# Block products for the first feed-forward matrix, on normalised rows, and the last norm's squares summed on VectorE

## The chip, the cores and the metric

The kernel runs on one core of a Trainium2 chip. The core has a matrix engine (TensorE, PE in the profile, with PEld for its weight loads), a vector engine (VectorE, DVE), an activation engine (ScalarE, ACT), GpSimd (POOL), and queues that issue DMAs (SP is SyncE's). The metric is the device time of one execution in microseconds; three runs of the kernel before gave 1327.4, 1327.84 and 1328.44 us, median 1327.84 us.

## What is computed

One step of a decoder layer in float32, for 512 prompt rows and 8 sample rows, 520 columns together. The change concerns the end of it:

```python
h = h + mix                                   # mix: everything up to w_o
h = h + swiglu(rmsnorm(h, ln2_g), w_ffn_in, w_ffn_out)
y = rmsnorm(h, lnf_g)

def swiglu(xn, w_ffn_in, w_ffn_out):
    a, b = split(xn @ w_ffn_in, 2)            # each 2816 wide = 22 blocks of 128
    return (silu(a) * b) @ w_ffn_out          # model width 1024 = 8 blocks of 128
```

## The kernel before

**Layout.** Activations stand transposed: model channels on the 128 partitions, in 8 blocks `c`, and 520 columns in two halves of 260 (`HF`). A float32 product is made of three products of a rounded high part and a remainder: weight high by data high, weight high by data low, weight low by data high (`product`, L237). Weights arrive in 194 tiles of eight 128x128 blocks (`raw`, 512 KB, four buffers); ScalarE copies 512 columns into the high part `wh` (L195), VectorE subtracts for the low part `wl` (L198). This is done five such blocks ahead of their use (`AHEAD`, called from `advance`).

**A unit.** `unit` (L252) multiplies 8 weight blocks with a full tile: 8 x 3 x 2 halves = 48 matmuls of 260 columns, into a pair of PSUM banks `pm`, of which there are two (tag `pm`, used in turn). After each `k`, `pump` lets side generators emit one piece of work and runs work put off with `later(n, ...)` by n pumps. Order in each engine's queue is the order in which the program emits; nothing is re-sorted.

**A quad.** `quad` (L266) does two output blocks against eight input blocks by seven block products instead of eight (Strassen's scheme in Winograd's form): seven blocks `j`, each 4 x 3 matmuls, 84 in all. Seven sums of weights are made on VectorE by `block_sum` (1024, 512 and 512 columns), seven high and low parts are split, and the right side's four sums come from `right` (L292): four VectorE operations of 260 columns, one ScalarE copy of 1820 columns, and a VectorE subtraction of 1820 columns put off by three pumps. Three banks are used: bank 0 for j = 0, 2, 4, 6, bank 1 for j = 1, 5, and `pc` for j = 3. After j = 0, 1, 2, 4 ScalarE copies the bank to a side tile (`snap`, L289), because the next block product is accumulated on top of it. So j = 2 may not start before the copy after j = 0 has read the bank, j = 4 not before that after j = 2, j = 6 not before that after j = 4.

**The feed forward before.** `ffn_in(i)` makes hidden block i of 22: one unit for `a`, one for `b`, on `X2`, which is h times the norm's gain, split in two, *without* the row factor. The factor `rs2` (1/rms of each column) is applied when the banks are read: VectorE multiplies `a` (L1209), ScalarE takes Silu (L1210), VectorE multiplies `b` (L1215) and the two (L1220). Every odd i up to 15 then runs `right` on the pair; blocks 17 to 21 are split plainly (`whole`, L1201). `ffn_out(c)` multiplies the hidden blocks with the second matrix, by quads, for two chunks of eight hidden blocks; the third chunk of six is plain. The order is: hidden 0 to 8, four quads, hidden 9 to 16, four quads, hidden 17 to 21, the plain end. `rs2` itself comes from `gen_norm2`, which runs under the first units: VectorE has both halves of it late in the second unit.

**The end.** The third chunk's output is first made for c = 0 to 3 whole, then for c = 4 to 7 half by half. `gen_final(c)` squares h (ScalarE), transposes h on TensorE (`fin_T`, three transposes), sums squares with three small matmuls against a column of ones (`fin_ss`, L1277 and L1279), and VectorE multiplies the transposed rows by the gain (`fin_g`, L1283). In the last half, after the first matmuls of c = 6, everything pending is drained and `fin_out(0)` finishes the first half of the rows; `fin_out(1)` ends the program.

Of the kernel before, what the change touches and what calls it, by code (L numbers as in the profile page):

```python
# [27 lines left out]
QUADS = {s + 2 * i: 4 for s in (146, 170) for i in range(4)}  # L28
# [4 lines left out]
def tile_hybrid_layer(  # L33
# [204 lines left out]
    def product(pm, n, k, nk, src, fs):  # L238
        h, l = split[bid[n // 8, n % 8 // 4]]
        j = n % 4  # L240
        wh, wl = h[:, j * 128:(j + 1) * 128], l[:, j * 128:(j + 1) * 128]
        xh, xl = src(k)
        for w, x, first, last in ((wh, xh, k == 0, False), (wh, xl, False, False), (wl, xh, False, k == nk - 1)):
            for f in fs:
                PE.matmul(pm[:, f, :HF], w, x[:, f * HF:(f + 1) * HF], start=first, stop=last)  # L245
# [4 lines left out]

    def unit(nk, src, evac=None):
        pm = pmain.tile([128, 2, 512], F32, tag="pm", name="pm")  # L252
# [13 lines left out]
    def quad(odd, xh, xl, snap, evac):  # L266
# [5 lines left out]
        pms = [pmain.tile([128, 2, 512], F32, tag="pm", name="pm")[:, 0, :HF] for _ in range(2)]  # L272
        out = (pms[::-1] if odd else pms) + [None]
# [162 lines left out]
    for h in range(RH):  # L436
# [245 lines left out]
        for which in ("q", "k"):  # L682
            e0, e1 = rot(which)
            if h == 0 and which == "q":
                pattern[:] = ["P"]
                push("P", gen_norm1())
                pms = [pmain.tile([128, 2, 512], F32, tag="pm", name="pm") for _ in range(2)]
# [482 lines left out]

    def gen_norm2():
# [10 lines left out]
        for f in range(2):  # L1182
# [3 lines left out]
            yield  # L1186


    pattern[:] = ["P"]
    push("P", gen_norm2())  # L1190

    UH = bpool.tile([128, 28, HF], F32R, tag="bg", name="UH")
    UL = fp.tile([128, 28, HF], F32R, name="UL")
    UF = fp.tile([128, 8, HF], F32, name="UF")
    UH4, UL4 = (u.rearrange("p (k x) c -> p k x c", x=7) for u in (UH, UL))
    UHp, ULp = (u.rearrange("p (k f) c -> p k (f c)", f=2) for u in (UH, UL))
    NP = CHUNKS[2][0]

# [4 lines left out]

    def ffn_in(i):
        s = {}

        def ev_fa(pm, s=s):
            t = ftmp("fa")
            V.tensor_tensor(halves(t), pm, halves(rs2), op=ALU.mult)  # L1209
            A.activation(t, t, AF.Silu)  # L1210
            s["a"] = t

        def ev_fb(pm, i=i, s=s):
            t = ftmp("fb")
            V.tensor_tensor(halves(t), pm, halves(rs2), op=ALU.mult)  # L1215
            if i > NP:
                V.tensor_tensor(t, t, s["a"], op=ALU.mult)
                whole(i, halves(t))
                return
            V.tensor_tensor(UF[:, 1:3, :] if i % 2 else UF[:, 0::7, :], halves(t), halves(s["a"]), op=ALU.mult)  # L1220
            if i % 2:
                k = i % 8 // 2
                right(UF, UH4[:, k], UL4[:, k])

        pa = unit(8, lambda k: (X2[:, k, :], X2[:, 8 + k, :]), ev_fa if i else None)
        pb = unit(8, lambda k: (X2[:, k, :], X2[:, 8 + k, :]), ev_fb if i else None)
        if i == 0:
            drain("P")
            ev_fa(pa)
            ev_fb(pb)  # L1230

    def ffn_out(c):

        s12 = fp.tile([128, 2, HF], F32, tag="s12", bufs=2, name="s12")
        s35 = fp.tile([128, 2, HF], F32, tag="s35", bufs=2, name="s35")
# [14 lines left out]
        quad(c // 2 % 2, UH4, UL4, [s12[:, 0, :], s12[:, 1, :], s35[:, 0, :], s35[:, 1, :]], evac)  # L1250

    for (a, n), ahead in zip(CHUNKS, (1, 1, 0)):
        if not ahead:
            whole(NP, UF[:, 0::7, :])
        for i in range(a and a + 1, a + n + ahead):
            ffn_in(i)
        if ahead:
            for c in range(0, 8, 2):
                ffn_out(c)

    yt = bpool.tile([128, 4, D], F32, tag="bx", name="yt")
    ys = fp.tile([4, 2, D], F32, name="ys")
    gb = fp.tile([128, D], F32, name="gb")
# [11 lines left out]
    def fin_ss(c, f, sq):  # L1275
        for j in range(2):
            PE.matmul(ssb[:, 2 * f + j:2 * f + j + 1], sq[:, 128 * j:128 * j + 128], ones1, start=c + f + j == 0, stop=c == 7,  # L1277
                      skip_group_check=True)
        PE.matmul(ssb[:4, 4 + f:5 + f], sq[:, HT:HF], ones1, start=False, stop=c == 7, skip_group_check=True)  # L1279
# [6 lines left out]

    def gen_final(c, fs=(0, 1)):
        sq = ftmp("sqf")
        A.activation(sq[:, :HF * len(fs)], hT[:, c, HF * fs[0]:HF * fs[-1] + HF], AF.Square)
        for f in fs:  # L1290
            for _ in range(2 if f else 4):
                yield
            a = fin_T(c, f)
            fin_ss(c, f, sq[:, HF * (f - fs[0]):])
            yield
            fin_g(c, f, *a)
            if f != fs[-1]:
# [32 lines left out]
    pms = [pmain.tile([128, 2, 512], F32, tag="pm", name="pm") for _ in range(2)]  # L1330
    base = pos[0]
    for i, (c, k) in enumerate(LAST):
# [3 lines left out]
        if k == nk - 1:  # L1336
            ev_f(pms[c][:, :, :HF], c)
            push("P", gen_final(c))
    pos[0] = base + len(LAST)
    for c in (2, 3):  # L1340
        unit(nk, usrc, lambda pm, c=c: ev_f(pm, c))
        push("P", gen_final(c))
    base = pos[0]
    for f in range(2):
        for c in range(4, 8):
            o = pmain.tile([128, 2, 512], F32, tag="pm", name="pm")[:, :1, :]
            for k in range(nk):
# [10 lines left out]
                if f and c == 6 and k == 0:  # L1358
# [3 lines left out]
            if c < 7:  # L1362
                push("P", gen_final(c, (f,)))
# [44 lines left out]
def _layout(np, i):  # L1408
# [14 lines left out]
    ffi = ff[[j for c in range(NFF) for j in (c, NFF + c)]].reshape(NFF, 16, 128, 128)  # L1423
    fo = _tiles(f["w_ffn_out"][0])

    def quad(w, c, a):
# [37 lines left out]
```

## Time and profile before

| what | value |
|---|---|
| median of three runs | 1327.84 us |
| the profiled execution | 1326.3 us, of it span 1324.5 us |
| VectorE busy, 20 us from 1073 to 1083 and 1043 to 1053 | 4.17 and 9.07 us of 10 |
| first unit of the feed forward | from about 926.4 us |
| the four quads of the first chunk | about 1033 to 1074 us |
| those of the second chunk | about 1166 to 1206 us |
| plain end of the second product | from about 1264 us |
| last output DMA issued | about 1321 us |

The busy time of an engine says how much of a stretch it had an instruction in work; an engine can be far from full over the span and full in one stage. Each engine takes its queue in order, so an instruction that waits also holds what is behind it. The rows of the profile stand in the prediction, beside what is read from them.

### The profile page before, as it was taken

What the parts mean: (1) busy time and instruction counts of PE and PEld (TensorE: products, weight loads), DVE (VectorE), ACT (ScalarE), POOL (GpSimd) and SP (SyncE); (2) the same over time, 40 slices, a digit from 0 to 9 for tenths busy, and PEclk for the clock granted to TensorE, in tenths of its full rate; (3) what the DMA queues carried; (4) which work ended last, traced back from release to release, by engine and by line L of the source; (5) the groups of instructions that cost most, each with busy time, mean ns of one, the idle gap of its engine ahead of it and who ended that gap; (6) DMA issues with size and microseconds to landing.
All of it is one profiled execution on the core that took longest, in us unless ns stands there. A gap on an engine that the chain in (4) does not pass through costs nothing.

```text
span 1324.5 us, 25798 instructions
## 1 busy us (share of the span) xinstructions
PE 1303.2 (98%) x10681; PEld 1272.9 (96%) x10681; DVE 753.6 (57%) x1582; ACT 527.1 (40%) x984; POOL 83.6 (6%) x69
## 2 busy tenths in 40 slices
PE   8999999999999999999999999999999999999997
PEld 7999999998888999999999999999999999999997
DVE  7867636747655532234545455486455865586443
ACT  4564334535553522243434433233333543354321
POOL 3601001001002000000000000040000000000000
PEclk9999999999999999999999999999999999999998
DMA  6266235746485233444645546534232333223211
GB/s 217 84 234 227 89 118 201 232 134 229 156 295 158 89 96 96 133 132 147 181 135 171 152 142 220 167 119 133 72 106 80 94 101 110 80 88 120 86 43 66
DMA packets 89782, 183.37 MB, mean 138 GB/s; under 512 B 12024, under 2 KB 33944, under 8 KB 89664
## 3 DMA queue, kind: packets, MB, share of 16 engines
q1 hardware_dynamic: 88944, 180.64, 42.7%
q8 instruction: 84, 1.38, 0.4%
q10 hardware_dynamic: 720, 1.07, 0.2%
q14 instruction: 34, 0.28, 0.1%
HBM read 155.70 MB, written 25.98 MB: 137 GB/s over the span
## 4 chain that ended last, share of the span: by engine, by line
PE 89%; DVE 4%; DMA 3%; issue 1%; ACT 1%; POOL 1%; SPq 0%; DVEq 0%; ACTq 0%
PE pm L245 70%; PE pm L283 5%; PE sp L308 3%; DMA vb<-vd 2%; PE sp L537 2%; PE sp L555 2%; PE pm L1355 2%; PE sp L947 1%; PE sp L489 1%; PE pc L283 1%; DVE wl L198 1%; PE sp L897 1%; PE sacc L1092 1%; DVE X L408 0%; PE sp L886 0%
## 5 line engine op out<-in xcount | busy, mean ns | idle before, releaser
L245 PE MATMUL pm<-X,wh 128*128 128x260 f32 x4608 | 755.9, 286 | 3.9 <-DVE X L340 3.6
L245 PEld LDWEIGHTS pm<-X,wh 128*128 128x128 f32 x4608 | 636.0, 189 | 18.2 <-issue 8.2
L245 PE MATMUL pm<-X,wl 128*128 128x260 f32 x2304 | 464.6, 283 | 0.0
L198 DVE TENSOR_TENSOR wl<-raw,wh 128x512 fp32r<-128x512 f32 x384 | 275.1, 720 | 209.0 <-ACT wh L195 206.9
L245 PEld LDWEIGHTS pm<-X,wl 128*128 128x128 f32 x2304 | 356.0, 189 | 0.0
L195 ACT ACTIVATE wh<-raw 128x512 fp32r<-128x512 f32 x384 | 237.9, 625 | 242.0 <-PE pm L245 186.0
L245 PE MATMUL pm<-GA,wh 128*128 128x260 f32 x512 | 82.2, 283 | 0.0
L245 PEld LDWEIGHTS pm<-GA,wh 128*128 128x128 f32 x512 | 70.1, 188 | 0.0
L317 POOL TENSOR_TENSOR r<-v,cst 128x4 f32<-128x4 f32 (+4 forms) x14 | 17.6, 1260 | 603.2 <-DVE v L315 603.2
L605 ACT ACTIVATE kv<-vb,ks 128x512 f32<-128x512 f32 x64 | 44.2, 714 | 27.9 <-DMA vb<-vd 27.5
L283 PE MATMUL pm<-UH,wh 128*128 128x260 f32 x192 | 54.4, 283 | 0.1
L283 PE MATMUL pm<-UH,wl 128*128 128x260 f32 x192 | 54.3, 283 | 0.0
L283 PE MATMUL pm<-UL,wh 128*128 128x260 f32 x192 | 54.3, 283 | 0.0
L640 DVE SCALAR_TENSOR_TENSOR st<-st,kv 128x512 f32<-128x512 f32 x64 | 45.4, 713 | 11.1 <-ACT kv L605 11.0
L245 PE MATMUL pm<-GA,wl 128*128 128x260 f32 x256 | 51.6, 283 | 0.0
L1210 ACT ACTIVATE fa<-fa 128x520 f32<-128x520 f32 x22 | 14.1, 639 | 71.3 <-DVE fa L1209 71.3
L245 PE MATMUL pm<-M,wh 128*128 128x260 f32 x256 | 41.1, 282 | 0.0
L245 PEld LDWEIGHTS pm<-GA,wl 128*128 128x128 f32 x256 | 39.5, 188 | 0.0
L283 PEld LDWEIGHTS pm<-UH,wh 128*128 128x128 f32 x192 | 36.2, 189 | 0.5 <-issue 0.5
L283 PEld LDWEIGHTS pm<-UL,wh 128*128 128x128 f32 x192 | 36.2, 188 | 0.0
L283 PEld LDWEIGHTS pm<-UH,wl 128*128 128x128 f32 x192 | 36.1, 188 | 0.0
L865 DVE SCALAR_TENSOR_TENSOR area<-area 128x128 f32<-128x128 f32 x96 | 22.7, 290 | 22.5 <-DMA area<-qd 22.5
(280 smaller groups left out, 1549.5 us busy)
## 6 DMA issues: line engine op xcount, KB each, us to landing
raw<-wall SPq DMA_DIRECT2D x192, 512.0 KB
st<-state SPq DMA_DIRECT2D x64, 256.0 KB
out<-st SPq DMA_DIRECT2D x64, 256.0 KB
area<-ck SPq DMA_DIRECT2D x24, 512.0 KB
vb<-vd SPq DMA_DIRECT2D x32, 256.0 KB
area<-qd SPq DMA_DIRECT2D x12, 512.0 KB
cb<-cd SPq DMA_DIRECT2D x4, 768.0 KB
xr<-xT SPq DMA_DIRECT2D x8, 260.0 KB
```

What stands on the lines that cost most here:

```text
L195: A.activation(h, r, AF.Copy)
L198: V.tensor_tensor(l, r, f32(h), op=ALU.subtract)
L245: PE.matmul(pm[:, f, :HF], w, x[:, f * HF:(f + 1) * HF], start=first, stop=last)
L283: PE.matmul(out[bank], w[:, ks], r[:, k, x, :], start=bank not in begun, stop=k == nkp - 1 and r is xh and w is l, skip_group_check=True)
L308: PE.transpose(out, in_, ident[:n, :n])
L317: G_.tensor_tensor(r[:rows, :ncol], v[:rows, :ncol], mhalf[:rows].to_broadcast([rows, ncol]), op=ALU.pow)
L537: PE.matmul(sp[:, i0:], v[x][:, jb, c * 128:(c + 1) * 128], scs[y][:, SCO[jb]:SCO[jb] + T - i0], start=jb == 0 and x == y, stop=jb == 3 an ...
L555: PE.matmul(sp, kt[x][:, jb, dt * 128:(dt + 1) * 128], v[y][:, jb, :], start=jb == 0 and x == y, stop=jb == 3 and x == 1)
L605: A.activation(kvs[i][:, :DV], vbs[b], AF.Copy, scale=ks[:, dt, b:b + 1])
L640: V.scalar_tensor_tensor(sts[i], sts[i], GAMMA[h], kvs.pop(i)[:, :DV], op0=ALU.mult, op1=ALU.add)
L865: V.scalar_tensor_tensor(pr[:, e], kb[:, e], 1.0, qb[:, e], op0=ALU.mult, op1=ALU.mult, accum_out=Ss[:, g, 32 * h + b:32 * h + b + 1])
L1355: PE.matmul(o[:, 0, :HF], w[:, js], x, start=k == 0 and i == 0, stop=k == nk - 1 and i == 2)
```

## The change

Twelve hidden blocks (5, 6, 8, 9, 11, 12, 14, 15, 17, 18, 20, 21) take `a` and `b` together by one `quad` (84 matmuls) in place of two units (96). For that the right side must be the eight input blocks in Winograd's form, and because the results of block products are subtracted from each other and read straight from PSUM, the rows are normalised beforehand: `gen_factors` makes `XH`/`XL` (7 + 1 slots for each of four pairs) from h, gain and `rs2`. Blocks 0 and 1 still run on `X2`, blocks 2, 3, 4, 7, 10, 13, 16, 19 run plainly on the plain slots of `XH`/`XL`, without the multiplication by `rs2`. `UH` moves to `X2`'s place, `XH` takes the place that `UH` had; the residual tiles `xr` now share a ring of five with the temporaries (two and six before); the tile `s35` has one buffer. At the end the squares are summed by VectorE into `ssa`, and only two sums per half go through TensorE; a final's transposes start two pumps after its block is complete, in consecutive pairs of pumps, and `fin_out(0)` stands three matmuls earlier. The host lays out the weights to match. The core of the diff:

```diff
+INQ = (5, 6, 8, 9, 11, 12, 14, 15, 17, 18, 20, 21)
+FFSEQ = []
+for (a_, n_), ahead_ in zip(CHUNKS, (1, 1, 0)):
+    FFSEQ += [("in", i_, i_ in INQ) for i_ in range(a_ and a_ + 1, a_ + n_ + ahead_)]
+    FFSEQ += [("out", c_, True) for c_ in range(0, 8, 2) if ahead_]
+QUADS = {128 + 2 * i_: 4 for i_, e_ in enumerate(FFSEQ) if e_[2]}
...
+    def free_pair():
+        turn["busy"] ^= 1
+        return bank_pair(turn["busy"])
...
+    def gen_factors():
+        yield from gen_norm2()
+        xs = {}
+        def one(c, out):
+            x = ftmp("xn")
+            V.scalar_tensor_tensor(x, hT[:, c, :], g2v[:, c:c + 1], rs2, op0=ALU.mult, op1=ALU.mult)
+            xs[c] = x
+            hi, lo = (u[:, c // 2, 1:3, :] if c % 2 else u[:, c // 2, 0::7, :] for u in (XH4, XL4))
+            A.activation(hi, halves(x), AF.Copy)
+            later(2, lambda: V.tensor_tensor(lo, halves(x), f32(hi), op=ALU.subtract))
+        for c in range(8):
+            one(c, None)
+            yield
+            yield
+        for k in range(4):
+            x1, x2 = xs.get(2 * k), xs.get(2 * k + 1)
+            if k < 3:
+                x1, x2 = ftmp("xn"), ftmp("xn")
+                for c, x in ((2 * k, x1), (2 * k + 1, x2)):
+                    V.scalar_tensor_tensor(x, hT[:, c, :], g2v[:, c:c + 1], rs2, op0=ALU.mult, op1=ALU.mult)
+                yield
+            t = fp.tile([128, 4, HF], F32, tag="ts", name="ts")
...
+            yield
+            hi, lo = XH4[:, k, 3:7, :], XL4[:, k, 3:7, :]
+            A.activation(hi, t, AF.Copy)
+            yield
+            yield
+            V.tensor_tensor(lo, t, f32(hi), op=ALU.subtract)
+            yield
...
         def ev_fa(pm, s=s):
             t = ftmp("fa")
-            V.tensor_tensor(halves(t), pm, halves(rs2), op=ALU.mult)
-            A.activation(t, t, AF.Silu)
+            if i < NX:
+                V.tensor_tensor(halves(t), pm, halves(rs2), op=ALU.mult)
+                A.activation(t, t, AF.Silu)
+            else:
+                A.activation(halves(t), pm, AF.Silu)
...
+    def ffn_in_quad(i):
+        s12, s35 = snaps()
+        t = ftmp("fa")
+        def evac(j, bank):
+            if j in (3, 5):
+                f = (j - 3) // 2
+                V.tensor_tensor(t[:, f * HF:(f + 1) * HF], bank, s12[:, f, :], op=ALU.add)
+                if f:
+                    A.activation(t, t, AF.Silu)
+            elif j == 4:
+                later(1, lambda: V.tensor_tensor(s35[:, 0, :], s35[:, 0, :], s35[:, 1, :], op=ALU.add))
+            elif j == 6:
+                def mult(out):
+                    for f, x in ((1, s35[:, 0, :]), (0, bank)):
+                        V.scalar_tensor_tensor(out[:, f, :], x, -1.0, t[:, f * HF:(f + 1) * HF], op0=ALU.mult, op1=ALU.mult)
+                middle(i, mult)
+        quad(XH4, XL4, [s12[:, 0, :], s12[:, 1, :], s35[:, 0, :], s35[:, 1, :]], evac)
...
+    def fin_sum(c, fs):
+        o = slice(HF * fs[0], HF * fs[-1] + HF)
+        if c == 0:
+            A.activation(ssa[:, o], hT[:, c, o], AF.Square)
+        else:
+            sq = ftmp("sqf")[:, :HF * len(fs)]
+            A.activation(sq, hT[:, c, o], AF.Square)
+            later(2, lambda: V.tensor_tensor(ssa[:, o], ssa[:, o], sq, op=ALU.add))
...
-                if f and c == 6 and k == 0:
+                if f and c == 5 and k == 5:
                     drain("P")
                     fin_out(0)
```

`middle(i, mult)` runs `mult` into `UF` and, for odd i from 3 to 15, at once `right`; for i above 16 it runs `mult` into a temporary and `whole`. For i = 1, `right` runs in the main loop right after the block.

More of the change, by code (lines that the diff above doesn't have):

```diff
@@ L244, in product @@
             for f in fs:
-                PE.matmul(pm[:, f, :HF], w, x[:, f * HF:(f + 1) * HF], start=first, stop=last)
+                PE.matmul(pm[:, f, :HF], w, x[f] if isinstance(x, tuple) else x[:, f * HF:(f + 1) * HF], start=first, stop=last)
     def begin(n):
@@ L264, in tile_hybrid_layer, with quad @@
     SEVEN = ((0, 0), (1, 3), (0, 4), (2, 1), (0, 5), (1, 2), (0, 6))
-    def quad(odd, xh, xl, snap, evac):
+    def quad(xh, xl, snap, evac):
         s = pos[0] // 8
@@ L270, in quad @@
         nkp = QUADS[s]
-        pms = [pmain.tile([128, 2, 512], F32, tag="pm", name="pm")[:, 0, :HF] for _ in range(2)]
-        out = (pms[::-1] if odd else pms) + [None]
+        turn["busy"] ^= 1
+        pms = {}
+        for _ in range(2):
+            i = turn["next"]
+            pms[i] = bank_pair(i)[:, 0, :HF]
+        out = [pms[turn["busy"]], pms[1 - turn["busy"]], None]
         begun = set()
@@ L1202, in whole, with middle @@
         later(2, lambda: V.tensor_tensor(lo, t, f32(hi), op=ALU.subtract))
+    def middle(i, mult):
+        if i > NP:
+            t = halves(ftmp("fu"))
+            mult(t)
+            whole(i, t)
+            return
+        mult(UF[:, 1:3, :] if i % 2 else UF[:, 0::7, :])
+        if i % 2 and i > 1:
+            k = i % 8 // 2
+            right(UF, UH4[:, k], UL4[:, k])
     def ffn_in(i):
@@ L1216, in ev_fb @@
[L1216 to L1226, printed above, removed]
+            if i < NX:
+                t = ftmp("fb")
+                V.tensor_tensor(halves(t), pm, halves(rs2), op=ALU.mult)
+                pm = halves(t)
@@ L1248, in evac @@
                 V.tensor_tensor(h2[:, 0, :], h2[:, 0, :], bank, op=ALU.subtract)
-        quad(c // 2 % 2, UH4, UL4, [s12[:, 0, :], s12[:, 1, :], s35[:, 0, :], s35[:, 1, :]], evac)
-    for (a, n), ahead in zip(CHUNKS, (1, 1, 0)):
-        if not ahead:
-            whole(NP, UF[:, 0::7, :])
[L1255 to L1263, printed above, removed]
+        quad(UH4, UL4, [s12[:, 0, :], s12[:, 1, :], s35[:, 0, :], s35[:, 1, :]], evac)
+    for kind, i, seven in FFSEQ:
+        if kind == "out":
+            ffn_out(i)
+            continue
+        if i == NP + 1:
+            whole(NP, UF[:, 0::7, :])
+        (ffn_in_quad if seven else ffn_in)(i)
+        if i == NX - 1:
+            UH = bpool.tile([128, 28, HF], F32R, tag="bx", name="UH")
+            UH4, UL4 = (u.rearrange("p (k x) c -> p k x c", x=7) for u in (UH, UL))
+            UHp, ULp = (u.rearrange("p (k f) c -> p k (f c)", f=2) for u in (UH, UL))
+            right(UF, UH4[:, 0], UL4[:, 0])
+    last = bpool.tile([128, 7 * D], F32, tag="bg", name="last")
+    yt = last[:, :4 * D].rearrange("p (j c) -> p j c", j=4)
+    ys = last[:4, 4 * D:6 * D].rearrange("p (f c) -> p f c", f=2)
+    gb = last[:, 6 * D:]
     SP.dma_start(gb, lnf.to_broadcast([128, D]))
@@ L1362, in tile_hybrid_layer @@
             if c < 7:
-                push("P", gen_final(c, (f,)))
+                finals(c, (f,))
+    run_delayed(True)
     drain("P")
```

101 lines of the change are left out of this document (61 added, 40 removed).

## The prediction

> **What bounds the kernel now.** I read the page's shares first, then the chain that ended last, then busy times by stretch, then the queues of the engines in order of time.
>
> ```profile
> span 1324.5 us, 25798 instructions
> PE 1303.2 (98%) x10681; PEld 1272.9 (96%) x10681; DVE 753.6 (57%) x1582; ACT 527.1 (40%) x984; POOL 83.6 (6%) x69
> ...
> PE 89%; DVE 4%; DMA 3%; issue 1%; ACT 1%; POOL 1%; SPq 0%; DVEq 0%; ACTq 0%
> ```
>
> TensorE is in work for 98% of the span and holds 89% of the chain: less TensorE work is time gained as long as nothing else is late. Next, two stretches of the feed forward (busy us of PE, PEld, DVE, ACT, POOL; clock; DMA), and, from TensorE's queue, the last matmul of a quad's block j = 0, the first of j = 1, and the first of the next quad:
>
> ```profile
> 1043.00:1053.00 10.00, 10.00 (x86) 10.00 (x84) 9.07 (x17) 5.53 (x11) 0.00 (x0) 1.00 0.37 107
> 1073.00:1083.00 10.00, 10.00 (x85) 10.00 (x85) 4.17 (x8) 3.05 (x6) 0.00 (x0) 1.00 0.35 105
> ...
> 1034.46 0.28 PE L283 MATMUL pm<-UH,wl 128*128 128x260 f32 x1
> 1034.79 0.36 PE L283 MATMUL pm<-UH,wh 128*128 128x260 f32 x1
> 1043.51 0.28 PE L283 MATMUL pm<-UH,wh 128*128 128x260 f32 x1
> ```
>
> In a quad VectorE is in work 9.07 us of 10, in a plain stretch 4.17. TensorE loses nothing in either. From 1034.79 to 1043.51 lie 72 matmuls: 0.121 us each, 0.120 in longer runs. A block j is thus 1.44 us, a quad 10.1, a unit of 48 matmuls 5.76.
>
> **Removed: matmuls.** Twelve hidden blocks fall from 96 matmuls to 84. 12 x 12 x 0.120 = 17.3 us less, if TensorE stays the bound.
>
> **Moved: the last norm's squares.** From the chain of the plain end, and TensorE's queue around the drain, with the granted clock (the number before the DMA share):
>
> ```profile
> 1276.33 0.33 PE sp L308 x3
> 1276.66 0.34 PE ssb L1277 x4
> 1277.12 3.06 PE pm L245 x24
> 1280.17 0.33 PE sp L308 x3
> ...
> 1301.10 0.49 PE L308 MATMUL sp<-cst,hT 128*128 128x128 f32 x3
> 1309.14 0.58 PE L1355 MATMUL pm<-UH,wh 128*128 128x260 f32 x1
> 1315.62 0.49 PE L308 MATMUL sp<-cst,hT 128*128 128x128 f32 x3
> ...
> 1306.00:1308.00 2.00, 2.00 (x20) 1.81 (x18) 1.22 (x4) 0.00 (x0) 0.00 (x0) 0.94 0.00 0
> 1312.00:1314.00 2.00, 2.00 (x11) 2.00 (x11) 0.43 (x1) 0.42 (x1) 0.00 (x0) 0.50 0.88 318
> ...
> 1311.03 0.73 DVE L1316 TENSOR_SCALAR ys<-ys,r 4x1024 f32<-4x1024 f32 x1
> L245 PE MATMUL pm<-UH,wh x48: 278/282/389, 1264.3 to 1283.3; 128*128 128x260 f32 x48
> ```
>
> From one final to the next are 3.84 us for 24 matmuls (2.88): a final costs 0.96, of which the sums are 0.34 plus 0.12 (two L1279 matmuls, an estimate by the L1277 rate), so 0.50 without them. The drain takes 8.0 us for eight finals (1301.10 to 1309.14), after which the clock is 0.50 and the last 33 matmuls take 6.5 us instead of 4.0. Before, from 1264.3 (the first matmul on UH there, the row above) to 1315.6: 51.4 us. After: 288 x 0.120 = 34.6; a wait for the first bank, 0.4 as now (what the terms before leave over); fourteen finals inside the stream at 0.50 = 7.0, because four pumps per final now do where eight did; the sums and transposes of the first half 1.4; no drain and so no low clock. That is 43.4, 8.0 less. Against it stands 0.9: the bank of c = 5 is read behind the final scaling on VectorE, which waits for GpSimd and ends now 2.6 after the drain (1311.03 + 0.73 - 1309.14); with 0.43 for the read that is 3.0, and the bank is due after 18 matmuls, 2.2. I take 7.1 less; bounds 5 (side banks late) and 8.5. VectorE's added sums are 0.6 us each at half load and cost nothing; if they were late, only the last one would count, 0.7.
>
> **Added: the factors, in VectorE's queue.** Rows for the durations: ScalarE's and VectorE's groups (the mean ns of one stands behind the bar), and VectorE's queue, where starts lie closer than durations.
>
> ```profile
> L299 DVE TENSOR_TENSOR UL<-UF,UH 128x1820 fp32r<-128x1820 f32 x8 | 16.4, 2049 | 0.0
> L298 ACT ACTIVATE UH<-UF 128x1820 fp32r<-128x1820 f32 x8 | 13.8, 1730 | 43.2 <-DVE UF L297 43.2
> L1210 ACT ACTIVATE fa<-fa 128x520 f32<-128x520 f32 x22 | 14.1, 639 | 71.3 <-DVE fa L1209 71.3
> ...
> 1042.72 0.42 DVE L1246 TENSOR_TENSOR hT<-hT,s 128x260 f32<-128x260 f32 x1
> 1043.05 0.69 DVE L185 TENSOR_TENSOR qq<-raw 128x512 f32<-128x512 f32 x1
> 1043.65 0.69 DVE L198 TENSOR_TENSOR wl<-qq,wh 128x512 fp32r<-128x512 f32 x1
> 1044.26 0.42 DVE L1248 TENSOR_TENSOR hT<-hT,pm 128x260 f32<-128x260 f32 x1
> 1046.70 1.22 DVE L179 TENSOR_TENSOR qq<-raw,raw 128x1024 f32<-128x1024 f32 x1
> 1047.83 0.69 DVE L198 TENSOR_TENSOR wl<-raw,wh 128x512 fp32r<-128x512 f32 x1
> ...
> 939.51 0.43 DVE L1185 COPY rs<-sp 128x260 f32<-128x260 f32 x1 [0.59 <-PE sp L323]
> 940.82 0.72 PE L245 MATMUL pm<-X,wh 128*128 128x260 f32 x4
> ```
>
> So in a full queue 260 columns cost 0.34, 512 or 520 cost 0.61, 1024 cost 1.13, 1820 about 1.97; 1040 is estimated at 1.15. `rs2` is whole at 939.9; the second unit ends at 940.8. From there VectorE must, in this order, up to the four sums of pair k = 1: eight scalings of 520 (5.0) and eight remainders (4.9), the three products of block 0 and of block 1 (4.1), `right` of pair 0 (four of 260 in a chain, 1.5), five weight remainders (3.0), UL's remainder (2.0), pair 0's two scalings, four sums and remainder (1.2 + 1.45 + 1.15), pair 1's scalings and sums (1.2 + 1.45): 27.0 us. It also waits some 2.4 us for ScalarE's copies between a scaling and its remainder, and 2.4 for the UF copy (1.73) and the weight copy behind it. That ends at 971.7. ScalarE then does the copy of the sums (1.0) and only behind it Silu of block 2's first unit (0.64): the bank is free at 973.3. Without waits TensorE would want it, at the third block's first unit, 940.8 + 4 x 5.76 = 963.9. The next unit wants its bank at 969.6; VectorE reads it after pair 1's remainder, pair 2 (scalings, sums, a wait, remainder), two weight remainders and pair 3's sums, at 982.3. After that VectorE has caught up. **Loss 12.7 us.** Low end 6.7: were every wait for ScalarE hidden, the 4.9 and the 1.1 in pair 2 fall off. High end 14.5: 0.43 per 260 columns in chains in place of 0.34, some 20 of them. The first weight blocks are five ahead (over 14 us) and aren't what waits.
>
> **Added: sevens in a row, and ScalarE's copy.** The copy that frees a bank, its normal time, and the end of a pair of hidden blocks as it runs now:
>
> ```profile
> 1034.77 0.39 ACT L289 ACTIVATE s<-pm 128x260 f32<-128x260 f32 x1 [0.60 <-PE pm L283]
> 1022.54 0.70 DVE L1220 TENSOR_TENSOR UF<-fb,fa 128x520 f32<-128x520 f32 x1
> 1023.16 0.42 DVE L294 TENSOR_TENSOR UF<-UF 128x260 f32<-128x260 f32 x1
> 1024.76 1.73 ACT L298 ACTIVATE UH<-UF 128x1820 fp32r<-128x1820 f32 x1 [5.39 <-DVE UF L297]
> 1026.39 0.61 ACT L195 ACTIVATE wh<-qq 128x512 fp32r<-128x512 f32 x1
> 1026.91 0.62 ACT L195 ACTIVATE wh<-raw 128x512 fp32r<-128x512 f32 x1
> ```
>
> The bank copy comes 0.2 us after the matmuls' nominal end and takes 0.39, so it has 0.84 us to spare before j = 2 needs the bank. At an odd hidden block, product (1022.54), sums and UH copy (1024.76) end with ScalarE free at 1026.39: 3.85 us in which ScalarE takes nothing else, and two weight copies then follow at once. Before, a plain unit comes next, and nobody misses it. Now a seven follows in four places.
> - 7 to 8 and 13 to 14: 0.2 + 3.85 + one weight copy 0.52 + 0.39 + 0.05 = 5.0 after the unit's end; j = 2 is due at 2.9: **2.1 lost**, twice.
> - 5 to 6 and 11 to 12: the product waits longer. At the end of j = 5 VectorE adds (0.42), ScalarE does Silu (0.64) and the weight copy, VectorE its remainder, then two products of 260: the second ends 1.9 after the quad's end instead of 1.2 (the row at 1044.26, 0.75 after 1043.51, plus 0.42). Bank 0 is the next one's bank 1, due at 1.44: 0.5 lost. Then four sums, copy, weight copy, bank copy end at 6.1 against 2.9: **3.2 lost** in all, twice.
> - 8 to the output quads and 14 to 15: UL's remainder (2.0) and the weight sums (1.13 + 0.61) have put VectorE behind, a bank copy stands behind a weight copy that waits for a sum (0.6), the add and the two products come late (0.4 and 1.1): **2.1 lost**, twice.
> - 17 to 18 and 20 to 21: only the 0.5, twice. Behind 2, 3, 4, 9, 10, 12, 15, 16 and 19 I find none.
>
> Sum 4.2 + 6.4 + 4.2 + 1.0 = **15.8 us**. Low end 8.6: the four copies at 2.1 and no knock-on. The DMAs go past unharmed: the same tiles in the same order, and a seven's pair is asked for 7 us before its first sum. `gb` now waits for the last seven, some 8 us ahead of its first use.
>
> **A clock rule.** TensorE had two lone matmuls, each after about 1 us of nothing, before those of 334.02, and the clock was halved after it:
>
> ```profile
> 330.78 0.50 PE L489 MATMUL sp<-ph,pl 128*128 128x512 f32 x1 [0.97 <-ACT pl L476]
> 332.28 0.49 PE L489 MATMUL sp<-ph,pl 128*128 128x512 f32 x1 [1.00 <-DVE ph L477]
> 334.02 1.32 PE L489 MATMUL sp<-ph,pl 128*128 128x512 f32 x4 [1.24 <-DVE pl L477]
> ...
> 336.00:338.00 2.00, 2.00 (x8) 2.00 (x8) 0.51 (x2) 0.83 (x2) 0.00 (x0) 0.50 1.03 376
> ```
>
> The 6.8 us wait in the factor stage should do the same; half speed over about 3.3 us costs 1.7, which the bank wait that follows hides. For waits of 2 to 3 us this row decides nothing. [...]
>
> **The sum.** -17.3 - 7.1 + 12.7 + 15.8 = +4.1 us on the profiled execution's 1326.3, so 1330.4; the median of the three runs stands 1.5 above that execution, so **1332.0**.
>
> **Rivals.**
> - *The UH copy holds no bank* (the other side). If ScalarE's bank copies get done in time because the sums and the copy end inside the slack, only the six waits of 0.5 stay: 15.8 becomes 3, and the time 1319. It decides at a chain under 2.9 us from a unit's end to the bank copy's end. For it: quads of today lose nothing. Against: the 3.85 us are measured, in a queue kept in order. 0.20.
> - *The factors hide*. If VectorE keeps up until block 3, 12.7 becomes about 0: 1319. It decides at 29.7 us of work between 939.9 and 969.6; I count 36 up to the last read. For it: half of VectorE is idle in plain stretches. 0.16.
> - *Clock halved by short waits*: four times 1.7 on top, 1339. 0.14.
> - *It doesn't save matmul time*: the new right sides or pairs of slices run slower than 0.120. At 0.123 over the 1,800 matmuls of the first product the loss is 5 more, 1337. Nothing in the profile speaks for it. 0.05.
> - The forecast as worked: 0.45, by itself 1326 to 1338.
>
> **Range and chances.** Low ends of both losses give 1318, high ends with the clock 1341; 1318 to 1341 leaves out under 2 in 10 (both rivals that gain at once, 1306). 0.2% (2.7 us) is about what a measurement can tell from none. Faster: the first two rivals, 0.36. Within: the lower part of the forecast, 0.17. Slower: 0.28 of the forecast, the clock and the matmul rival, 0.47.
>
> **What would show it.** In the profile after: 144 matmuls of 260 columns less; TensorE idle some 7 us and 3 us at the third plain block, released by ScalarE's Silu and VectorE's product; idle of 2 to 3 us inside the sevens of 6, 8, 12 and 14 at j = 2, released by L289's copy, which stands behind a copy of 1820 columns; no clock of 0.50 near the end, and the finals apart. I am wrong if TensorE runs through these sevens, or if its wait at block 3 is under 3 us.

## The result, and the profile after

The changed kernel takes 1334.62 us (median; 1333.82 to 1335.39), the kernel before in the same runs 1327.37 us: ratio 1.0069, interval 1.0048 to 1.009 (the two medians alone give 1.0055). The forecast was 1332.0. The profiled execution took 1334.04 us, 7.7 us more than that of before (span 1332.2 against 1324.5). From the page:

```profile
span 1332.2 us, 25611 instructions
PE 1285.9 (97%) x10465; PEld 1251.6 (94%) x10465; DVE 818.0 (61%) x1713; ACT 570.6 (43%) x1080; POOL 83.3 (6%) x69
...
PE 84%; DVE 7%; DMA 3%; issue 3%; ACT 2%; POOL 1%; SPq 1%; DVEq 0%; ACTq 0%
```

TensorE has 17 us less in work, VectorE 64 us more and ScalarE 44 us more, and the chain that ended last has given up five points of TensorE. Where TensorE stood still from the feed forward's start on is told by the view of waits (its queue, 926 to 1340 us: waiting line, releaser, us in total, times, longest):

```profile
PE pm L306 <- ACT s L312: 9.4, 6, 2.3
PE pm L250 <- ACT fa L1296: 5.4, 1, 5.4
PE pm L250 <- DVE fb L1302: 2.7, 1, 2.7
PE pm L306 <- DVE UF L1331: 2.4, 4, 0.9
PE pm L250 <- DVE UF L1304: 1.5, 1, 1.5
PE sp L331 <- DVE hT L1443: 1.3, 1, 1.3
PE pm L306 <- DVE fu L1331: 0.6, 2, 0.3
PE pm L250 <- DVE fa L1293: 0.5, 1, 0.5
PE pm L250 <- ACT XH L1230: 0.3, 1, 0.3
PE pm L250 <- DVE XL L1231: 0.2, 1, 0.2
```

L306 is the matmul of the block products (a seven, below, is a quad: seven of them): twelve waits there, 12.4 us, for a bank copy (`s`) or for the products (`UF`, `fu`). L250 is the plain unit: six waits, 10.6 us, all in the factor stage. One more is at the end. A wait costs some 0.27 more than its idle time: the idle time counts only from 0.28 us after the start of the last matmul before it, where the next one would have started after 0.12, and the second matmul behind the wait starts 0.22 instead of 0.12 after the first. Four rows of TensorE's queue cut the span: the first matmul of the feed forward (before, then after), the first of the first block product on `XH`, and the first of the plain end.

```profile
926.48 0.64 PE L245 MATMUL pm<-X,wh 128*128 128x260 f32 x4
```

```profile
928.01 0.64 PE L250 MATMUL pm<-X,wh 128*128 128x260 f32 x4
...
1003.68 0.28 PE L306 MATMUL pm<-XH,wh 128*128 128x260 f32 x1
...
1280.40 0.40 PE L250 MATMUL pm<-UH,wh 128*128 128x260 f32 x2
```

Before, hidden block 5 began at about 987.0 (940.82 + 8 units of 5.77) and the plain end at 1264.3. So:

| stretch | before, us | after, us | difference |
|---|---|---|---|
| up to the feed forward, nothing changed | 926.5 | 928.0 | +1.5 |
| hidden blocks 0 to 4 | 60.5 | 75.7 | +15.2 |
| block 5 to the plain end | 277.3 | 276.7 | -0.6 (-17.3 of matmuls, +16.7 of stalls) |
| plain end | 60.2 | 51.8 | -8.4 |

The first line can't be laid to the change: the matmuls there are the same, and in the profiled executions of the ten experiments below the feed forward begins anywhere from 924.69 to 928.79. The three others were forecast at +12.7, -1.5 and -7.1.

**The factor stage.** TensorE's queue at the waits of hidden blocks 1 to 3 (start, duration, idle before and its releaser), then ScalarE's queue and VectorE's at block 0:

```profile
943.01 0.71 PE L250 MATMUL pm<-X,wh 128*128 128x260 f32 x4 [0.54 <-DVE fa L1293]
960.08 0.50 PE L250 MATMUL pm<-XH,wh 128*128 128x260 f32 x2 [0.32 <-ACT XH L1230]
960.82 0.51 PE L250 MATMUL pm<-XL,wh 128*128 128x260 f32 x2 [0.23 <-DVE XL L1231]
964.26 0.80 PE L250 MATMUL pm<-XH,wh 128*128 128x260 f32 x2 [2.69 <-DVE fb L1302]
977.06 0.80 PE L250 MATMUL pm<-XH,wh 128*128 128x260 f32 x2 [5.38 <-ACT fa L1296]
986.36 0.51 PE L250 MATMUL pm<-XH,wh 128*128 128x260 f32 x2 [1.52 <-DVE UF L1304]
```

```profile
942.95 1.28 ACT L1294 ACT_TABLE_LOAD   x1
944.24 0.64 ACT L1294 ACTIVATE fa<-fa 128x520 f32<-128x520 f32 x1
```

```profile
944.91 0.70 DVE L1304 TENSOR_TENSOR UF<-fb,fa 128x520 f32<-128x520 f32 x1 [1.44 <-ACT fa L1294]
```

The last wait, at 986.36, decides: from there the remaining three units run through to 1003.68. VectorE sets it, and near its start it stands 1.44 us for a Silu that is itself behind a table load.

**A seven after an odd block.** In time order, block 5 to block 6: TensorE's wait at j = 1, then VectorE's last sum of `right`, ScalarE's queue, and TensorE's wait at j = 2:

```profile
1015.70 0.39 PE L306 MATMUL pm<-XH,wh 128*128 128x260 f32 x1 [0.32 <-DVE UF L1331]
1019.72 0.39 PE L306 MATMUL pm<-XH,wh 128*128 128x260 f32 x1 [2.33 <-ACT s L312]
```

```profile
1016.70 0.42 DVE L320 SCALAR_TENSOR_TENSOR UF<-UF 128x260 f32<-128x260 f32 x1
```

```profile
1017.15 1.72 ACT L321 ACTIVATE UH<-UF 128x1820 fp32r<-128x1820 f32 x1 [2.92 <-DVE UF L320]
1018.78 0.61 ACT L200 ACTIVATE wh<-qq 128x512 fp32r<-128x512 f32 x1
1019.30 0.37 ACT L312 ACTIVATE s<-pm 128x260 f32<-128x260 f32 x1
```

ScalarE is idle for 2.92 us, waiting for the sums that its head instruction needs, then copies 1820 columns, then a weight block, and only then the bank for which TensorE has been waiting.

**The end.** From the chain of waits, then TensorE's queue at the one wait left:

```profile
1294.06 0.33 PE sp L331 x3
1294.39 1.45 PE pm L250 x12
```

```profile
1319.75 0.55 PE L331 MATMUL sp<-cst,hT 128*128 128x128 f32 x3 [1.32 <-DVE hT L1443]
```

Finals are now apart, three transposes to twelve matmuls, with no drain of eight in a row.

### The profile page after: what moved, and what is told of

It is laid out like the page before. It is cut to its first block, busy times and chain, and to the rows that moved or that the text cites. A ratio compares the mean times of both kernels' runs of the same rounds, so it can differ in the third digit from the quotient of the medians.

```text
span 1332.2 us, 25611 instructions
## 1 busy us (share of the span) xinstructions
PE 1285.9 (97%) x10465; PEld 1251.6 (94%) x10465; DVE 818.0 (61%) x1713; ACT 570.6 (43%) x1080; POOL 83.3 (6%) x69
## 4 chain that ended last, share of the span: by engine, by line
PE 84%; DVE 7%; DMA 3%; issue 3%; ACT 2%; POOL 1%; SPq 1%; DVEq 0%; ACTq 0%
PE pm L250 58%; PE pm L306 11%; PE sp L331 3%; PE pc L306 2%; DMA vb<-vd 2%; PE sp L560 2%; PE sp L578 2%; DVE wl L203 1%; PE pm L1474 1%; PE sp L970 1%; PE sp L512 1%; ACT wh L200 1%; PE sp L920 1%; PE oacc L673 1%; PE sacc L1115 1%
## 5 line engine op out<-in xcount | busy, mean ns | idle before, releaser
L250 PE MATMUL pm<-X,wh 128*128 128x260 f32 x3328 | 550.7, 287 | 4.7 <-DVE X L363 3.6
L250 PEld LDWEIGHTS pm<-X,wh 128*128 128x128 f32 x3328 | 460.5, 189 | 19.4 <-issue 8.3
L203 DVE TENSOR_TENSOR wl<-raw,wh 128x512 fp32r<-128x512 f32 x384 | 275.0, 720 | 165.6 <-ACT wh L200 162.0
L250 PE MATMUL pm<-X,wl 128*128 128x260 f32 x1664 | 336.2, 284 | 0.0
L250 PEld LDWEIGHTS pm<-X,wl 128*128 128x128 f32 x1664 | 257.8, 189 | 0.4 <-DVE wl L373 0.4
L306 PE MATMUL pm<-XH,wh 128*128 128x260 f32 x288 | 83.2, 289 | 11.6 <-ACT s L312 9.4
L250 PE MATMUL pm<-GA,wh 128*128 128x260 f32 x512 | 82.2, 283 | 0.0
L306 PE MATMUL pm<-XL,wh 128*128 128x260 f32 x288 | 81.8, 284 | 0.0
L306 PE MATMUL pm<-XH,wl 128*128 128x260 f32 x288 | 81.6, 283 | 0.0
L250 PEld LDWEIGHTS pm<-GA,wh 128*128 128x128 f32 x512 | 70.1, 188 | 0.0
L306 PEld LDWEIGHTS pm<-XH,wh 128*128 128x128 f32 x288 | 54.5, 189 | 14.1 <-ACT s L312 10.6
L250 PE MATMUL pm<-XH,wh 128*128 128x260 f32 x256 | 53.2, 290 | 9.9 <-ACT fa L1296 5.4
L306 PE MATMUL pm<-UH,wh 128*128 128x260 f32 x192 | 54.4, 283 | 0.9 <-DVE UF L1331 0.9
L306 PEld LDWEIGHTS pm<-XL,wh 128*128 128x128 f32 x288 | 54.7, 190 | 0.0
L306 PEld LDWEIGHTS pm<-XH,wl 128*128 128x128 f32 x288 | 54.6, 190 | 0.0
L306 PE MATMUL pm<-UL,wh 128*128 128x260 f32 x192 | 54.2, 282 | 0.0
L203 DVE TENSOR_TENSOR wl<-qq,wh 128x512 fp32r<-128x512 f32 x60 | 41.2, 687 | 21.1 <-ACT wh L200 20.8
L306 PE MATMUL pm<-UH,wl 128*128 128x260 f32 x192 | 54.1, 282 | 0.0
```

The source lines that it names most:

```text
L203: V.tensor_tensor(l, r, f32(h), op=ALU.subtract)
L250: PE.matmul(pm[:, f, :HF], w, x[f] if isinstance(x, tuple) else x[:, f * HF:(f + 1) * HF], start=first, stop=last)
L306: PE.matmul(out[bank], w[:, ks], r[:, k, x, :], start=bank not in begun, stop=k == nkp - 1 and r is xh and w is l, skip_group_check=True)
```

## Experiments

Edits are against the changed kernel unless said otherwise. Ratios are to the kernel before, which ran beside each.

**1. The end alone.** The kernel before, with only the new end: `fin_sum`, `finals`, `fin_ss` on two sums, and `fin_out(0)` in c = 5.

```diff
-            push("P", gen_final(c))
+            finals(c)
...
-                if f and c == 6 and k == 0:
+                if f and c == 5 and k == 5:
```

> The kernel before with only the last norm's part of the change: squares summed on VectorE, transposes in pairs of pumps, first half finished three matmuls earlier; all products of the first matrix plain, no normalised rows. My account (the end of the program read off the two traces: 60.2 us before, 51.8 after): 8 us less than before, 1319 to 1320 us, and no granted clock of 0.50 before the last transposes. If the gain at the end came from the sevens instead (data ready earlier, another bank order), this run stays within 2 us of before.

Measured: 1317.7 us, ratio 0.9934 (0.9919 to 0.9949), so 8.8 us less. The end is a gain by itself, somewhat larger than expected (1319 to 1320). From the feed forward's start on, its only wait is the one that the changed kernel has too:

```profile
PE sp L308 <- DVE hT L1334: 1.3, 1, 1.3
```

**2. ScalarE's long copy later.** It is put three pumps back, behind the bank copies of the next seven's start, and the remainder behind it.

```diff
-        A.activation(hi, t[:, 0:7, :], AF.Copy)
-        later(3, lambda: V.tensor_tensor(lo, t[:, 0:7, :], f32(hi), op=ALU.subtract))
+        later(3, lambda: A.activation(hi, t[:, 0:7, :], AF.Copy))
+        later(6, lambda: V.tensor_tensor(lo, t[:, 0:7, :], f32(hi), op=ALU.subtract))
```

> The changed kernel with ScalarE's copy of 1820 columns put off by three pumps and its remainder by six, so that in a seven that follows the bank copy after j = 0 stands ahead of it. My account: the waits of 2.2 to 2.6 us at j = 2 in the sevens of 6, 8, 12 and 14 go (9.6 us, and the low clock in 12, 1.6); the later waits in 8 and 14 (2.1 each) are VectorE's and may stay: 1323 to 1326 us. If VectorE's load is the bound inside the sevens and ScalarE's copy only the last to arrive, the wait moves to the products on VectorE and the time stays above 1331.

Measured: 1320.65 us, ratio 0.9954 (0.9939 to 0.997): 14 us less than the changed kernel, more than expected (1323 to 1326). Its view of waits:

```profile
PE pm L306 <- DVE UF L1331: 2.4, 4, 0.9
...
PE pm L306 <- ACT s L312: 0.5, 2, 0.2
```

The waits for the bank copy fall from 9.4 to 0.5 us, those for the products stay. That shows the mechanism: nothing but the place of one ScalarE instruction and its remainder was changed. Four of the six waits are gone, worth some 10.0 us (8.9 idle and 0.27 each), and so is the low clock behind one of them, 1.6 (below): from block 5 to the plain end the trace has 265.39 us instead of 276.71. In the profiled execution the factor stage is 1.1 us shorter too (74.60 instead of 75.67).

**3. The factors spread out.** Seven pumps of nothing ahead of each of the four pairs, so that VectorE gets to the products in between.

```diff
         for k in range(4):
+            for _ in range(7):
+                yield
```

> The changed kernel with seven more pumps ahead of each of the four pairs of the normalised rows' sums, so that they end just before the first seven and not in block 3. My account: the waits of 2.7, 5.4 and 1.5 us at blocks 2 and 3 and the low clock behind them were VectorE's and ScalarE's queues in the wrong order, not too much work over five blocks; they go but for 3 to 5 us: 1322 to 1326 us. If VectorE is simply full until the first seven, the waits come back in blocks 3 and 4 and the time stays above 1331.

Measured: 1333.44 us, ratio 1.0054 (1.004 to 1.0068). A miss: no gain beyond the interval (expected were 1322 to 1326). TensorE's queue shows the stall moved, not gone: up to block 5 the trace has 70.68 us instead of 75.67, from there to the plain end 282.04 instead of 276.71.

```profile
972.71 0.80 PE L250 MATMUL pm<-XH,wh 128*128 128x260 f32 x2 [6.25 <-ACT fa L1298]
1002.89 0.39 PE L306 MATMUL pm<-XH,wh 128*128 128x260 f32 x1 [3.57 <-DVE UF L1306]
```

The work put off comes due at the first seven, whose bank VectorE then reads late. So putting the work off alone doesn't help; whether VectorE's time up to block 5 is what is short, experiment 9 tests.

**4. Both.** Edits 2 and 3 together.

> Both edits together: ScalarE's copy of 1820 columns later, and the four pairs of sums spread. My account: the two losses are apart in time and add up, so the gains do too: 1311 to 1317 us, less than before and less than the kernel before with only the end changed. If they share a cause (VectorE's total), the gain is that of the larger alone, about 1323.

Measured: 1317.52 us, ratio 0.9928 (0.9914 to 0.9942), just above the expected range (1311 to 1317). Spreading gives some 3 us here; the intervals don't tell that from the 1 or 2 that it gives alone. The feed forward's part of the change now costs nothing over the end alone (0.9934), but gains nothing either.

**5. No sevens.** All hidden blocks plain, but factors, normalised rows and the new end kept.

```diff
-INQ = (5, 6, 8, 9, 11, 12, 14, 15, 17, 18, 20, 21)
+INQ = ()
```

> The changed kernel with the list of sevens empty: normalised rows, their sums and the new end are all there, every hidden block from 2 on runs plainly on the normalised rows. It prices the factor stage alone against the kernel with only the end changed (1317.7 us). My account: 13 to 16 us more, 1331 to 1334, with the waits of 2.7, 5.4 and about 1.5 us at blocks 2 and 3 as in the changed kernel, and none after; the twelve sevens of the change then save about as much in matmuls (17.3) as their own waits cost (17.4). If the loss at blocks 2 and 3 comes from the weight sums of the sevens to come, this run lies at 1318 to 1324.

Measured: 1331.59 us, ratio 1.0029 (1.0017 to 1.004), as expected. Against the end alone, the factor stage costs 0.0095, 12.6 us (10 to 15 by the two intervals). In the trace it takes 75.68 us up to block 5, as in the changed kernel (75.67): the other account, that the weight sums of the sevens to come make this loss, falls. Against the changed kernel, twelve sevens are worth +0.004, 5 us of loss (2 to 8.5 by the intervals; 3.0 by the medians): the matmuls that they save don't pay for their stalls. (In the traces, block 5 to the plain end takes 275.69 without them and 276.71 with them, only 1.0 more; but the profiled execution without sevens, 1333.66, is the slowest of its six.) The longest wait of the factor stage is that of the changed kernel:

```profile
PE pm L250 <- ACT fa L1296: 5.3, 1, 5.3
```

**6. The table load alone.** A Silu of one column ahead of the factors, so that the load is done before block 0's product needs it.

```diff
+    A.activation(warm, warm, AF.Silu)
     def gen_factors():
```

> The changed kernel with one more ScalarE instruction: Silu of one column, before the factors are made, so that the activation table is loaded ahead of the first unit's Silu instead of between the products of block 0. Theory (the load of 1.28 us stands in VectorE's chain, which sets the start of block 3): at least 1.3 us less than the changed kernel, 1331 to 1333.3 us, and VectorE's first product of block 0 no longer waits about 1.4 us for Silu. Up to 2 us more would go with it if a wait of TensorE falls so far that its clock isn't halved. Rival (the load is hidden by VectorE's wait for the copy of the first scaled rows, which comes at the same time): no change, 1334 to 1335 us.

Measured: 1333.1 us, ratio 1.0051 (1.0036 to 1.0065), in the range of the theory, but the interval overlaps that of the changed kernel. The trace settles it. VectorE's product waits 0.16 instead of 1.44 us, and the last wait of the list above comes earlier (VectorE's queue, then TensorE's):

```profile
942.89 0.70 DVE L1306 TENSOR_TENSOR UF<-fb,fa 128x520 f32<-128x520 f32 x1 [0.16 <-ACT fa L1296]
```

```profile
942.27 0.71 PE L250 MATMUL pm<-X,wh 128*128 128x260 f32 x4 [0.53 <-DVE fa L1295]
...
984.33 0.51 PE L250 MATMUL pm<-XH,wh 128*128 128x260 f32 x2 [1.06 <-DVE UF L1306]
```

From 942.27, where this kernel's second hidden block starts, that is 42.06 us; in the changed kernel, from 943.01 to 986.36, 43.35. The table load costs 1.3 us of the stage. That it hardly shows in the time of this execution has its reason behind the stage: from block 5 to the plain end it took 278.11 us instead of 276.71, as one wait more in the sevens was followed by a low clock (last section).

**7. The low part alone.** The remainder of a summed weight block (L203) one pump later, so that VectorE doesn't stand behind ScalarE's high part when a seven's products come due.

```diff
-        later(2, low)
+        later(3 if blocks[b][0] == "q" else 2, low)
```

> The changed kernel with the low part of the summed weight blocks put off by three pumps instead of two, and nothing else. Theory (TensorE's waits for VectorE's products at j = 1 of a seven, 3.0 us in all, come from VectorE standing in a low part that waits for ScalarE's high part, so that the sum and the products behind it are late): these waits go, and the rest of the waits for ScalarE's bank copy stay or shrink by what the products come earlier, so 3 to 6 us less than the changed kernel: 1328.5 to 1331.5 us. Rival (what counts in the sevens is only ScalarE's copy of 1820 columns, and the wait at j = 1 returns as a longer one at j = 2): within 1 us of the changed kernel, 1333.5 to 1335.5 us.

Measured: 1326.72 us, ratio 0.9998 (0.9983 to 1.0012): 8 to 9 us less than the changed kernel, more than the theory expected (3 to 6 less); the rival falls. Its view of waits:

```profile
PE pm L306 <- ACT s L312: 8.1, 4, 2.1
...
PE pm L306 <- DVE UF L1331: 0.2, 1, 0.2
```

Seven of the twelve waits at L306 are gone: five of the six for the products, and the two bank copies at 8 and 14 (0.41 each); the four long ones stay at 1.94 to 2.10. That is 4.1 us idle and 1.9 around it, and agrees with the theory. In the trace, block 5 to the plain end takes 271.87 us instead of 276.71: about the 6.0, less the 1.6 of a low clock after one wait more. The factor stage took 1.5 us longer there (77.20 instead of 75.67), though its waits are 1.0 shorter, with more low clock in it (matmuls 0.22 us apart also from 967.55 to 969.72, and again from 987.32 on). So the profiled execution, 1330.74, is only 3.3 us faster than that of the changed kernel. This program's twelve executions spread from 1322.76 to 1331.37, and their mean granted clock goes with it: 0.992 in the four fastest (to 1324.93), 0.987 in the three slowest (from 1328.37), the profiled one among them. Where the others lost less is on no trace; what the 8 to 9 have beyond the 6.0 is within the intervals.

**8. Both, with two more.** Edit 4, the early Silu, and the last drain where c = 5's last bank has been read, so that it isn't read behind the final scaling.

```diff
-                if f and c == 5 and k == 5:
-                    drain("P")
-                    fin_out(0)
             ev_f(o[:, :, :HF], c, f)
+            if f and c == 5:
+                drain("P")
+                fin_out(0)
```

> The kernel with both edits, and two small ones: ScalarE's table for Silu loaded ahead by an operation on one column, so that the load (1.28 us) isn't between block 0's products, and the first half of the rows finished behind the read of the bank of c = 5 and not before it. My account: the wait of 1.3 us at the end goes, the table's 1.3 goes from VectorE's queue, of which the bank wait at block 3 shows most: 1314 to 1316. If VectorE's queue is full anyway, only the 1.3 of the end shows: 1316.

Measured: 1313.94 us, ratio 0.9903 (0.9888 to 0.9918), at the fast end of what was expected. Against edit 4, the traces show both parts: feed forward to plain end 335.8 us instead of 337.0, and 50.4 instead of 51.8 behind it. The factor stage's waits are 5.0 and 2.4 us here, at blocks 3 and 5.

**9. First seven at block 6.** Edit 8 with block 5 plain, and the pairs spread over the time that this gives.

```diff
-INQ = (5, 6, 8, 9, 11, 12, 14, 15, 17, 18, 20, 21)
+INQ = (6, 8, 9, 11, 12, 14, 15, 17, 18, 20, 21)
...
+            for _ in range(8 if k else 11):
+                yield
```

> The same with eleven sevens, hidden block 5 plain, and the four pairs of sums spread over blocks 2 to 5, each copy placed behind the bank reads. The spread alone had moved the waits and not removed them: up to the first seven VectorE has more work than the stretch holds. My account now: with 11.5 us more stretch and one seven less (1.4 us of matmuls given back) the waits of 5.1 and 1.4 us and the low clock behind them (1.7) go: 1307 to 1311. If VectorE's order and not its amount was the limit, one block more doesn't help: 1315 to 1318.

Measured: 1311.9 us, ratio 0.9882 (0.9868 to 0.9895), 0.9 above the expected range (1307 to 1311), but well below the 1315 to 1318 of the other account, that order and not amount was VectorE's limit. One seven fewer costs 1.4 us of matmuls and takes a wait of 5.0 us away; in the two traces, feed forward to plain end is 4.4 us shorter (331.4 instead of 335.8). One long wait of the factor stage is left, beside one of 0.5 (the second line is of the sevens):

```profile
PE pm L250 <- DVE UF L1308: 2.4, 1, 2.4
PE pm L306 <- DVE UF L1335: 2.1, 3, 0.9
```

**10. With the low part later.** Edit 9 and edit 7.

> The same again, with the weights' low part in sevens put off by one pump more (three for two), so that the two products at the end of a seven stand ahead of it in VectorE's queue. My account: the waits at j = 1 behind a seven (0.6 to 1.2 us with their restart, eight places) come from VectorE waiting for ScalarE's weight copy, which stands behind Silu; they go, 4 to 5 us less than the run before. If the products wait for TensorE's own end and not for VectorE's queue, nothing moves (within 1 us).

Measured: 1306.05 us, ratio 0.9837 (0.9824 to 0.9851), 5.9 us less than edit 9 (4 to 5 expected) and faster than both kernels. What is left of waits in the feed forward:

```profile
PE pm L250 <- DVE UF L1308: 2.5, 1, 2.5
PE pm L250 <- DVE fa L1297: 0.5, 1, 0.5
PE pm L306 <- DVE UF L1335: 0.4, 2, 0.2
```

Of the sevens' waits 0.4 us remain of 12.4. With eleven of the twelve block products, what decided for them was the place of three instructions in the queues of ScalarE and VectorE. Feed forward to plain end now takes 327.0 us where the plain one of experiment 1 takes 337.8: eleven sevens save 15.8 us of matmuls, and the factor stage still costs 4.7 (65.26 up to block 5 instead of 60.53).

## Why the prediction was right, and where it was off

The time (1334.62 in a range of 1318 to 1341), the sign and the place of each large term came out. By its own steps, on the profiled executions:

| step | forecast, us | measured, us |
|---|---|---|
| 144 matmuls fewer | -17.3 | -17.3 |
| the end | -7.1 | -8.4 in the traces, -8.8 alone |
| factors, blocks 1 to 3 | +12.7 | +15.2 in the trace, +12.6 (10 to 15) by experiment 5 |
| sevens in a row | +15.8 | +16.7 with the clock, in the trace |
| ahead of the change | 0 | +1.5, between executions |

The parts of the sum were partly off in opposite ways: on the profiled executions it came to +7.7 instead of +4.1, with 1.5 from ahead of the change, 2.5 more for the factors, 0.9 more for the sevens and 1.3 less at the end. That the forecast came within 2.6 us of the median is in part luck.

- *Matmuls.* TensorE has 10465 instead of 10681: the 144 and the sums taken off it at the end. At full clock the sevens run at 0.12 (1003.68 and the rows after it); the rival that they save no matmul time falls. But in block 12 they didn't run at full clock (0.50 from 1131.26 to 1134.67).
- *Sevens in a row.* Place by place, the loss measured from start to start of the matmuls: 5 to 6 and 11 to 12 lost 3.2 and 3.1 (forecast 3.2), 7 to 8 and 13 to 14 2.2 (2.1), 8 to out and 14 to 15 2.1 (2.1), 17 to 18 and 20 to 21 0.6 (0.5), and nothing anywhere else. With the 1.6 of clock that is 17.7; the 16.7 of the table is 1 less, spread over the steps of the other matmuls (0.1203 us each in the stretch before, 0.1199 in the sevens). The rows at 1016.70 to 1019.72 are the chain as it was worked out: sums, copy of 1820 columns, weight copy, bank copy. Experiment 2 shows it by moving the copy and its remainder, experiment 7 shows the other part, the products late behind a remainder. The rival that the copy holds no bank falls. The net of sevens and matmuls was forecast as a gain of 1.5 us; against the kernel before the trace shows 0.6, but experiment 5, the cleaner test, a loss of 5 (2 to 8.5). So the small gain is not borne out.
- *Factors.* The engine, the releasers (Silu, then the product) and the place were right, the size in the trace 2.5 us too small. The start of block 3's second unit was forecast at 982.3; it came at 986.36, or 984.9 without the 1.5 from before the change. VectorE's time was summed too small, by one term that is known and a rest. The three products of block 0 were costed as 2.0 us of VectorE, but it waits 1.44 in them, for Silu behind a table load of 1.28: 1.3 us by experiment 6. The load isn't in the row of before that gave Silu's 0.64, since that row groups only the ACTIVATEs. The other 1.2 us of VectorE's queue were not traced to one instruction. A wait that was not foreseen, 2.69 at 964.26, cost nothing more, as the one behind it was longer. TensorE's idle, forecast as some 7 and 3 us, came as 2.69, 5.38 and 1.52; the prediction's own times give 9.4 (973.3 less 963.9) and 3.2, which is what its loss of 12.7 needs, so the 7 and the 6.8 beside its rows on the clock were not worked out from them. The rival that the factors hide falls, and experiment 3 shows that even spread out they don't.
- *The clock.* The half clock after the long wait was foreseen, and that it hides in the next wait: the clock was 0.50 from 974.25 to 981.08, and TensorE still waits 1.52 after the slow unit that starts at 977.06. The estimate of about 3.3 us at half speed fits the trace of before, where the clock was 0.50 from 334.95 to 338.36, 3.41 us. For waits of 2 to 3 us the rows decided nothing: that the forecast counted no clock for them rested on no run, and the third rival gave 1.7 us to each of four. It happened at one of the four in the profiled execution, block 12, and cost 1.6 (at two of the four in experiments 6 and 7). So the forecast and this rival were both partly right; of the rival's 6.8 us, 1.6 came. Which waits were hit is told in the last section.
- *The end.* The sign of both parts was right: finals in the stream at 0.33 instead of 0.50 (the chain's rows from 1294.06), and one wait, foreseen at 0.9 on the bank of c = 5, found as 1.32 on the transposes that need what is read from it. The 0.50 for a final was taken from the difference of 0.96 and the sums, and so held 0.17 of other things; fourteen times that is 2.4 us. The longer wait takes 0.7 of it back (1.32 and 0.27 around it, against 0.9), and 0.4 was not placed.

## What to carry to other kernels

A saving of matmuls counts only as long as the banks come free (here 17.3 us saved stood against 16.7 of stalls), so for every bank walk the whole queue of the engine that frees it: the instruction at its head may wait for another engine and hold the one that matters (ScalarE idled 2.92 us at the head of its queue, and TensorE 2.33 for the bank copy behind). A long copy for later use belongs behind the short copies that free a bank now (the waits for these fell from 9.4 to 0.5 us), and a remainder that waits for another engine behind the products that free one (3.0 to 0.2 us). When a step needs an engine for longer than the other work covers (here VectorE, up to block 5), spreading only moved the stall to the next consumer (5.0 us less up to block 5, 5.3 more behind it); start that consumer later, or give the engine less.

## What the runs showed of the hardware

The clock halved behind some waits of 2 to 3 us and not behind others. In the changed kernel, two waits of 2.33 us in the same kind of place went apart: the first, up to 1019.72, left the clock at 1.00, the second, up to 1130.79, was followed by 0.50.

The traces show what differed. In the changed kernel's feed forward the clock was 0.50 from 964.00 to 967.41, from 974.25 to 981.08 and from 1131.26 to 1134.67 us: for 3.41 us, and once for 6.83, twice that. The three starts lie 10.25 and 157.01 us apart, which is about 3 and 46 times 3.41. So both waits are read in steps of that length, counted from these starts, and beside them the wait of 2.33 us of experiment 6 (from 1015.38 to 1017.71) in the place of the first (busy us of PE, PEld, DVE, ACT, POOL; clock; DMA share; GB/s; changed kernel, then experiment 6):

```profile
1015.21:1018.62 3.41, 1.86 (x14) 1.48 (x12) 1.88 (x6) 1.47 (x1) 0.00 (x0) 1.00 0.32 125
1018.62:1022.04 3.42, 2.32 (x19) 2.32 (x20) 2.61 (x3) 2.94 (x8) 0.00 (x0) 1.00 0.00 0
1022.04:1025.45 3.41, 3.41 (x30) 3.41 (x30) 3.32 (x8) 1.87 (x4) 0.00 (x0) 1.00 0.52 129
...
1127.85:1131.26 3.41, 1.08 (x10) 0.87 (x9) 1.10 (x3) 3.04 (x5) 0.00 (x0) 1.00 0.00 0
1131.26:1134.67 3.41, 3.41 (x18) 3.41 (x17) 3.40 (x4) 1.70 (x4) 0.00 (x0) 0.50 0.00 0
```

```profile
1014.16:1017.58 3.42, 1.22 (x11) 1.01 (x9) 1.11 (x4) 2.43 (x4) 0.00 (x0) 1.00 0.12 48
1017.58:1020.99 3.41, 3.28 (x15) 3.28 (x16) 3.41 (x4) 1.67 (x5) 0.00 (x0) 0.50 0.00 0
```

The first wait is cut by a step's end: TensorE idles 1.55 us in one step (the 0.32 of the wait before it included) and 1.10 in the next, and the clock stays at 1.00. The second lies within one step, 2.33 us, and the next step runs at 0.50. In experiment 6 the wait of the first place, as long as before, begins 1.22 us into its step instead of 2.18; 2.20 us of idle time fall into that step, and the clock is halved behind it. The place and the length are the same, only where the wait falls among the steps differs. So it is all through the changed kernel's trace from the feed forward's start to the plain end: of 99 steps at full clock, three had 2.33, 2.56 and 2.67 us of TensorE's idle time, and each was followed by a step at 0.50; the others had 1.55 or less, and none was. In the trace of before, none of the 99 steps of that stretch had more than 0.05, and all ran at 1.00. In experiment 7, its steps counted from the low clock that began at some 1130.60, a wait of 1.82 us, up to 986.45, lay within one step and was followed by matmuls 0.22 us apart instead of 0.12 (from 987.32). What lies between 1.55 and 1.82 was not shown, and all of this is read off these full-size matmuls alone.

The step at 0.50 from 1131.26 holds 18 matmuls where that from 1022.04 at 1.00 holds 30 (as the records count them, ends overlapping). From the end of the wait on, 72 matmuls took 10.30 us behind the second wait and 8.74 behind the first, so the low clock cost 1.55, the 1.6 above. In experiment 7 both waits of 2.10 us, up to 1020.55 and 1130.61, lay within one step but for a few hundredths, and were followed by it (0.50 from 1022 to 1024 and from 1132 to 1134); those of 1.94 were cut by a step's end, and the clock stayed at 1.00 (1046 to 1050, 1156 to 1158).

The spread of a kernel's times can't be laid to such waits alone. In the twelve executions of experiment 7 a mean clock of 0.992 or 0.987 stood beside 1322.76 to 1324.93 or 1328.37 to 1331.37 us, but the seventeen of the kernel before that ran beside them, which in its trace has no wait of TensorE in the feed forward, spread from 1322.56 to 1331.24 as well, at 0.997 to 0.989. A change worth a few us therefore needs several executions of each kernel, and a trace that shows the place.
